# Transposes through DRAM in a hybrid attention and retention step: other run lengths, queues and due times

## The chip, the cores and the metric

The kernel runs on one core of one Trainium2 chip. The metric is the device time of one execution in microseconds (us); smaller is better. A core has TensorE (PE, matrix products; PEld is its weight load), VectorE (DVE), ScalarE (ACT), GpSimd (POOL) and SyncE (SP), which work side by side and wait for each other through semaphores. Transfers are issued into a queue by SyncE, ScalarE or GpSimd and carried out by 16 DMA engines that all queues share. An engine works through its own instructions in order, so one that waits holds up what stands behind it.

## The reference

One layer is applied to 1024 frames of a new stream (the prompt) and to 16 new frames of each of 8 running streams (the sample, 128 rows in all). The frames are normalised and projected to queries, keys, values and gates of 8 stick-breaking heads and 8 retention heads of 128 columns each:

```python
z = q @ k.T * HEAD_DIM ** -0.5
log_beta = log_sigmoid(z)
log_keep = where(strict, log_sigmoid(-z), 0.0)
later = cumsum(log_keep, reverse=True) - log_keep
o_sb = where(strict, exp(log_beta + later), 0.0) @ v
...
scores = (q_r @ k_r.T) * intra
o_r = scores @ v_r + (q_r @ s) * decay_read
s_new = s * gamma ** n + (k_r * decay_write).T @ v_r
...
y = concat(head_rms_norm(o_sb) * g * silu(gate_sb), head_rms_norm(o_r) * g * silu(gate_r))
x = x + rms_norm(y @ w_out) * norm_post
```

In the sample, stick-breaking attention also reads a cache of 1024 old keys and values for each stream and head ("decode"). The new keys, values and retention states are results too. All is float32.

## The kernel before

**Products.** The large projections run as three products of split numbers: each operand is cut into a high and a low part (`split`, L135: ScalarE copies the high part, VectorE subtracts), and high x high, high x low and low x high are added. Weights come in pieces of 256 KB on SyncE's queue (`load_w` L216, `project_rows` L262; in the output stage L969) into four buffers, and are split into four more. All frames of a group are held in SBUF as the moving operand.

**Stages.** First the frames are normalised and turned (to about 120 us). Then two groups of heads follow: group 0 has prompt tiles 0 to 3 and the sample, and runs the decode job of each head; group 1 has prompt tiles 4 to 7, and its stick-breaking rows are up to 1024 keys long. In each group a loop goes over 8 heads and issues six projections for each (plus two wide ones for every pair). The output projection ends the kernel.

**Jobs and ticks.** Everything else of a head is written as generators, "jobs": `ret_branch` with `retention`, `sb_branch` with `stick_breaking`, `decode`, and `Out.finish`. The projections call `tick()` after a few products (in `products` after each of the three products of one slice: two matmuls in group 0, one in group 1). A tick counts a clock up and lets one job that is due go on to its next `yield`; the number yielded is the count of ticks until it is due again. These numbers are the constants `D_...` at the top; where there are two, the first holds for group 0 and the second for group 1. `drain(job)` ticks without products until a job has ended. In the output stage one product group makes `D_OUT`, 35, ticks. `place(inst)` ties an instruction's place behind the last product issued so far; it adds no semaphore. What is not placed is ordered by the compiler on its own reckoning, with the program's order as its priority, as soon as the buffer it writes is free there.

**Round trips.** TensorE's time is spared by transposing elsewhere. VectorE's transpose turns only blocks of 32 x 32, so a larger one goes through DRAM: `turn_out` (L452) stores a tile [128, k x 128] to DRAM as [k, 128, 128] in runs of 512 B; `turn_in` (L458) reads it back with four DMAs, one for each group of 32 partitions, in runs of 128 B, so that the blocks stand in their new places; a VectorE transpose then turns each block and writes its result contiguously. There are five kinds of these trips: the attention weights of a row (`s_be`, in `stick_breaking`: store and reads on GpSimd's queue), those of decode (`s_bd`, store on GpSimd's queue, reads on SyncE's), retention's keys (`s_rk`), and the finished heads of both kinds and of decode (`s_o`); the last two store on ScalarE's queue and read on SyncE's.

**Stick breaking.** For each of four rows of a head the products `z` (L563) give `kp` and `be`; GpSimd masks the diagonal block (L485), VectorE runs the scan (L496) and a product (L497), and the row is stored. The next row's step begins with the reads of this one; two steps on VectorE transposes it (L552) and TensorE multiplies it with the values (L588). Between them lie `D_ZP`, `D_TB` and `D_AV` ticks, and `D_TR` for the last two rows.

**Decode.** 16 pieces of the key cache are loaded (L617, four DMAs of 64 KB each, on GpSimd's queue, three buffers), transposed (L646) and multiplied (L636), `D_ZC` ticks a piece. Then come the trip of the weights (`D_ROW`, `D_DTO`, `D_DTI`, `D_DTR`) and eight pieces of the value cache (L655, 512 KB each, SyncE's queue) in four steps of `D_VC` ticks with two pieces each (L698). The six buffers of tag `kv` are shared by the transposed keys and the values; `load_v()` stands at seven places ahead of the first products.

**Retention.** `ret_branch` sends the keys through DRAM (`D_RO` ticks to the reads, `D_RI` to the transpose L819), scales them, and goes through the tiles `D_RET` ticks apart; L755 is the state's product.

Of the kernel before, what the change touches and what calls it, by code (L numbers as in the profile page):

```python
# [38 lines left out]
D_ZC = 13  # L39
D_ROW = 24  # L40
D_VC = 14
# [4 lines left out]
D_RET = (9, 6)  # L46
D_RO = (21, 23)
D_RI = (19, 26)
D_TO = (26, 23)
D_TB = (33, 33)  # L50
D_TI = (24, 26)
# [9 lines left out]
def tile_hybrid_step(  # L61
# [227 lines left out]
    with ExitStack() as s1:  # L289
# [162 lines left out]
        def turn_out(src, tag, q=nc.scalar):  # L452

            s = scr.tile([src.shape[1], P, P], F32, name=tag)
            q.dma_start(s.rearrange("k q c -> q k c"), src)
            return s

        def turn_in(s, raw, q):  # L458

            for i in range(4):  # L460
                place(q.dma_start(
                    raw[32 * i : 32 * i + 32, :].rearrange("p (k a) -> p k a", a=32),
                    s[:, :, 32 * i : 32 * i + 32].rearrange("k (j b) a -> b (k j) a", b=32),
                ))

        def row_tiles(n, kind):
            if n > 512:
                pool = ip if kind == "r" else zp
                kp = pool.tile([P, n + 1], F32, name="kp", tag=f"kp{kind}")
                be = pool.tile([P, n], F32, name="be", tag=f"be{kind}")  # L470
            else:
                both = zp.tile([P, 2 * n + 1], F32, name="kb", tag=f"{kind}p")
                kp, be = both[:, : n + 1], both[:, n + 1 :]
            nc.vector.memset(kp[:, n : n + 1], 1.0)
            return kp, be
# [26 lines left out]
        class Out:  # L502
# [5 lines left out]
            def done(self, i):  # L508
                sq = op.tile([P, P], F32, name="sq", tag="sq")
                nc.scalar.activation(sq, self.o[:, i, :], AF.Square, accum_out=self.ssq[:, i : i + 1])  # L510

            def finish(self, b, h, gT, oT, dst):
# [4 lines left out]
                s = turn_out(self.o, f"s_o{b}_{h}_{self.nt}")  # L517
                yield D_TO[phase[0]]
                flat = self.o.rearrange("p k d -> p (k d)")
                turn_in(s, flat, nc.sync)  # L520
                yield D_TI[phase[0]]
                n = self.nt * P
                if oT is not None:
                    place(nc.vector.transpose(oT[:, :n], flat))
                    nc.vector.scalar_tensor_tensor(
                        gT[:, :n], oT[:, :n], gains[:, b, h : h + 1], gT[:, :n], ALU.mult, ALU.mult
                    )
                else:
                    for i in range(self.nt):
                        c = slice(i * P, (i + 1) * P)  # L530
                        blk = op.tile([P, P], F32, name="oT", tag="oT", bufs=1)
                        place(nc.vector.transpose(blk, flat[:, c]))
                        nc.vector.scalar_tensor_tensor(
                            gT[:, c], blk, gains[:, b, h : h + 1], gT[:, c], ALU.mult, ALU.mult
                        )
                nc.scalar.dma_start(dst, gT[:, :n])
# [4 lines left out]
        def stick_breaking(tiles, h, q2, keys, rest):  # L541
            out = None
            todo = list(enumerate(tiles))
            lag, kinds = 2, ("psr" if todo[0][1] else ("kp", "be", "cp"))
            rows = []
            for step in range(len(todo) + lag):
                if 0 < step <= len(todo):
                    _, be, turned = rows[step - 1]
                    turn_in(turned, be, nc.gpsimd)
                if step >= lag:  # L550
                    kp, be, _ = rows[step - lag]
                    place(nc.vector.transpose(kp[:, : be.shape[1]], be))  # L552
                if step < len(todo):
# [43 lines left out]
        def decode(h, qs, rest):  # L597
# [15 lines left out]
            def load(m):  # L613
                s, j, c = chunk(m)
                kc = ip.tile([P, 512], F32, name="kc", tag="kc", bufs=3)
                for i in range(4):
                    place(nc.gpsimd.dma_start(  # L617
# [4 lines left out]
                    ))  # L622
# [48 lines left out]
            turned = turn_out(be.rearrange("p (k c) -> p k c", c=P), f"s_bd{h}", nc.gpsimd)  # L671
# [3 lines left out]
            turn_in(turned, be, nc.sync)  # L675
# [3 lines left out]
            place(nc.vector.transpose(kp[:, :n], be))  # L679
# [7 lines left out]
            for k in range(0, 8, 2):  # L687
# [3 lines left out]
                load_v()  # L691
# [21 lines left out]
            ends["d"] = Job(out.finish(0, h, rest["gs"], None, s_ys[h]), 2)  # L713
# [95 lines left out]
        def ret_branch(gi, g, h, rq, rk, rv, rg):  # L809
            nt = len(g["tiles"])  # L810
            rkn = ep.tile([P, 6, P], F32, name="rkn", tag="rkn")

            out = Out(nt, "ro")
            s = turn_out(rk[:, : nt * P].rearrange("p (k t) -> p k t", t=P), f"s_rk{gi}_{h}")
            yield D_RO[phase[0]]
            raw = out.o.rearrange("p k d -> p (k d)")
            turn_in(s, raw, nc.sync)
            yield D_RI[phase[0]]
            place(nc.vector.transpose(rkn.rearrange("p k d -> p (k d)")[:, : nt * P], raw))  # L819
# [5 lines left out]
            ends["r"] = Job(out.finish(1, h, rg, None, s_y[gi][H + h]), 2)  # L825

        def sb_branch(gi, tiles, h, q2, keys, kT, rest, ks):
# [17 lines left out]
            if gi == 0:  # L845
                nc.scalar.dma_start(s_k[h], kT)
# [12 lines left out]
            ends["p"] = Job(out.finish(0, h, rest["sg"], None, s_y[gi][h][:, : 4 * P]), 2)  # L859
# [304 lines left out]
```

## Time and profile before

| | |
|---|---|
| median of 3 runs | 2516.05 us (2508.36 to 2516.53) |
| the profiled execution | 2514.29 us, of which 2512.6 us from the first to the last instruction (the span) |
| mean granted TensorE clock | 0.975 |
| instructions | 40784 |
| DMA | 418.69 MB in 632650 packets, 187776 of them under 512 B |
| queue of SyncE / of GpSimd / of ScalarE | 285.99 MB / 80.80 MB / 49.30 MB |
| share of 16 DMA engines' span | 45.3% / 14.2% / 6.4% |

How to read the views that follow. A page gives the busy time of each engine as a share of the span; an idle engine costs nothing unless it is the one that the others wait for. A line such as `PE pa L588 <- DVE kb L552` in the view of waits says that TensorE's instruction of line 588, which writes `pa`, had waited for VectorE's of line 552; a `q` behind an engine (SPq, POOLq) is its sequencer, which issues DMAs. A line of the timeline gives start, duration, engine, line, operation, `out<-in`, a count, and in brackets the idle time before and what ended it. "To landing" is the time from the issue of a DMA to the arrival of its last byte. The granted clock is the share of TensorE's full speed that the chip allowed.

### The profile page before, as it was taken

Reading aid. Unit: us, or ns where it says so; the run is one execution under the profiler, and the core shown is the slowest. Engines: PE = TensorE matmul, PEld = TensorE weight load, DVE = VectorE, ACT = ScalarE, POOL = GpSimd, SP = SyncE. Lnnn points to the kernel's source line nnn. Section 1 sums busy time; section 2 is a strip of 40 time slices with the busy share of each in tenths; the row PEclk is TensorE's granted clock in tenths of the full one; section 3 lists DMA queues with packets and bytes.
Section 4 is the critical chain, followed back from the end, with each engine's and each line's share of the span. In section 5 each row is a group of like instructions: output and inputs, shape, how many; then the busy total and the mean of one; then the engine's idle time right before and its main releaser. Section 6 shows DMA issues by size and latency. Waiting matters only on the chain. (4 is left out here: it accounts for less than half of the span.)

```text
span 2512.6 us, 40784 instructions
## 1 busy us (share of the span) xinstructions
PE 2377.4 (95%) x14832; PEld 2121.9 (84%) x14832; DVE 1284.7 (51%) x2658; ACT 891.0 (35%) x1925; POOL 704.9 (28%) x1133
## 2 busy tenths in 40 slices
PE   7999898999989989898898999999999997999998
PEld 7999798888979979797677889889889886778787
DVE  7245454454344554445545564555554565464544
ACT  6332232323223232232324333343343443444343
POOL 2134444444434434353331221221211212000000
PEclk9999999998999989999899999999999999999999
DMA  6647867868587776778866556555555557666554
GB/s 233 171 129 164 177 153 171 183 163 167 124 185 172 177 151 152 165 178 193 191 177 160 144 159 151 141 155 136 159 143 144 150 146 180 202 220 201 180 181 139
DMA packets 632650, 418.69 MB, mean 167 GB/s; under 512 B 187776, under 2 KB 575360, under 8 KB 630016
## 3 DMA queue, kind: packets, MB, share of 16 engines
q1 hardware_dynamic: 525424, 285.99, 45.3%
q0 software_dynamic: 36608, 80.80, 14.2%
q10 hardware_dynamic: 70416, 49.30, 6.4%
q8 instruction: 116, 1.90, 0.3%
q14 instruction: 86, 0.70, 0.1%
HBM read 336.24 MB, written 79.69 MB: 166 GB/s over the span
## 5 line engine op out<-in xcount | busy, mean ns | idle before, releaser
L137 DVE TENSOR_TENSOR wl<-wr,wh 128x512 fp32r<-128x512 f32 (+1 forms) x576 | 395.6, 691 | 625.0 <-ACT wh L136 607.9
L230 PE MATMUL acc<-mh,wh 128*128 128x256 f32 (+2 forms) x2304 | 672.6, 344 | 11.3 <-ACT mh L136 6.1
L230 PE MATMUL acc<-ml,wh 128*128 128x256 f32 (+2 forms) x2304 | 675.1, 344 | 0.3 <-DVE ml L137 0.3
L230 PE MATMUL acc<-mh,wl 128*128 128x256 f32 (+2 forms) x2304 | 667.7, 342 | 0.8 <-DVE wl L137 0.8
L136 ACT ACTIVATE wh<-wr 128x512 fp32r<-128x512 f32 (+1 forms) x576 | 357.3, 625 | 778.4 <-PE acc L230 399.5
L230 PEld LDWEIGHTS acc<-mh,wh 128*128 128x128 f32 x2304 | 429.1, 191 | 51.5 <-issue 8.5
L617 POOL DMA_DIRECT2D kc<-cache_sb_k x512 | 330.8, 652 | 503.2 <-DVE kcT L646 263.5
L230 PEld LDWEIGHTS acc<-mh,wl 128*128 128x128 f32 x2304 | 429.2, 191 | 40.1 <-issue 10.5
L230 PEld LDWEIGHTS acc<-ml,wh 128*128 128x128 f32 x2304 | 429.3, 191 | 36.6 <-issue 7.9
L275 PE MATMUL accn<-whn,mh 128*128 128x256 f32 x1152 | 334.6, 290 | 0.5 <-DVE rk L315 0.4
L275 PE MATMUL accn<-wln,mh 128*128 128x256 f32 x1152 | 329.3, 286 | 0.0
L275 PE MATMUL accn<-whn,ml 128*128 128x256 f32 x1152 | 328.5, 286 | 0.0
L275 PEld LDWEIGHTS accn<-whn,mh 128*128 128x128 f32 x1152 | 222.9, 193 | 11.2 <-issue 7.9
L980 PE MATMUL a<-wl,mh 128*128 128x512 f32 (+1 forms) x576 | 220.9, 384 | 9.9 <-DVE wl L137 9.9
L275 PEld LDWEIGHTS accn<-wln,mh 128*128 128x128 f32 x1152 | 223.1, 194 | 4.1 <-issue 3.3
L275 PEld LDWEIGHTS accn<-whn,ml 128*128 128x128 f32 x1152 | 222.9, 194 | 2.1 <-issue 2.1
L981 PE MATMUL a<-wh,ml 128*128 128x512 f32 (+1 forms) x576 | 220.9, 384 | 0.0
L979 PE MATMUL a<-wh,mh 128*128 128x512 f32 (+1 forms) x576 | 218.8, 382 | 0.5 <-DVE so L591 0.5
L137 DVE TENSOR_TENSOR wln<-wrn,whn 128x512 fp32r<-128x512 f32 x128 | 87.7, 689 | 127.6 <-ACT whn L136 119.3
L136 ACT ACTIVATE whn<-wrn 128x512 fp32r<-128x512 f32 x128 | 80.7, 631 | 188.0 <-PE accn L275 74.5
L980 PEld LDWEIGHTS a<-wl,mh 128*128 128x128 f32 x576 | 109.0, 189 | 33.1 <-DVE wl L137 12.4
L836 POOL DMA_DIRECT2D out<-kn x64 | 41.7, 655 | 324.0 <-DVE ou L148 101.0
(203 smaller groups left out, 2750.7 us busy)
## 6 DMA issues: line engine op xcount, KB each, us to landing
wr<-w_in SPq DMA_DIRECT2D x384, 256.0 KB, 3.5
wr<-w_out SPq DMA_DIRECT2D x184, 256.0 KB, 3.5
wrn<-w_in SPq DMA_DIRECT2D x128, 256.0 KB, 3.2
kc<-cache_sb_k POOLq DMA_DIRECT2D x512, 64.0 KB, 4.2
vc<-cache_sb_v SPq DMA_DIRECT2D x64, 512.0 KB, 8.5
xt<-x_prompt SPq DMA_DIRECT2D x8, 1024.0 KB, 5.7
xr<-x_prompt SPq DMA_DIRECT2D x8, 1024.0 KB, 6.1
out<-out ACTq DMA_DIRECT2D x12, 512.0 KB, 2.9
```

Of the source, the lines that this page charges most:

```text
L136: nc.scalar.activation(hi, src, AF.Copy)
L137: nc.vector.tensor_tensor(lo, src, hi.bitcast(F32), ALU.subtract)
L230: last = nc.tensor.matmul(a[:, :m], lhs[:, j, :], rhs[w][:, j, o : o + m], start=(w == 0 and j == 0 and n == 0), stop=(w == KT // WQ - 1 a ...
L275: product[0] = nc.tensor.matmul(a, lhs[q][:, jj, ts], rhs[:, j, :], start=(w == 0 and j == 0 and n == 0 and t % 2 == 0), stop=(w == KT // ...
L617: place(nc.gpsimd.dma_start(kc[32 * i : 32 * i + 32, :].rearrange("p (k d) -> p k d", d=32), cache_k[0, 2 * c + j, s * 512 : (s + 1) * 512 ...
L836: nc.gpsimd.dma_start(k_prompt[0, 0, tiles[0] * P : (tiles[0] + 4) * P, h, ds].rearrange("(j b) a -> b j a", b=32), kn[q, : 4 * P].rearran ...
L979: nc.tensor.matmul(a[:, :width], hi[q][:, j, ts], wh, start=(k == 0), stop=False)
L980: nc.tensor.matmul(a[:, :width], hi[q][:, j, ts], wl, start=False, stop=False)
L981: product[0] = nc.tensor.matmul(a[:, :width], lo[q][:, j, ts], wh, start=False, stop=(k == KT - 1))
```

## The change

Each round trip is written the other way about. `turn_out` stores 32 columns at a time, in runs of 128 B, as [4k, 128, 32], always on GpSimd's queue, in pieces of at most 28 x 128 runs. `turn_in` reads with one DMA in runs of 512 B, and what remains of the permutation is done by VectorE's transpose, whose output is written with a step of four elements (`untangle`). The reads of stick-breaking rows go on SyncE's queue in group 0 and on GpSimd's in group 1; they are issued not at the start of the next step but `D_T1` ticks after its `z`. The stores of `s_y`, `s_ys` and `s_k` move from ScalarE's queue to GpSimd's. Half of each cached key piece is loaded on SyncE's queue; these loads are no longer placed behind a product, and have four buffers. One value load less stands ahead of the first value products. The due times are set anew. Some tiles move to other pools or lose a second buffer, and the rows' two tiles are no longer cut from one.

```diff
-D_ZC = 13
+D_ZC = 12
-D_VC = 14
+D_VC = 18
-D_RET = (9, 6)
-D_RO = (21, 23)
-D_RI = (19, 26)
-D_TO = (26, 23)
-D_TB = (33, 33)
-D_TI = (24, 26)
+D_RET = (7, 6)
+D_RO = (32, 30)
+D_RI = (30, 30)
+D_TO = (40, 40)
+D_T1 = (14, 14)
+D_T2 = (19, 19)
+D_TI = (30, 34)
...
-        def turn_out(src, tag, q=nc.scalar):
-
-            s = scr.tile([src.shape[1], P, P], F32, name=tag)
-            q.dma_start(s.rearrange("k q c -> q k c"), src)
+        def turn_out(src, tag):
+            m = src.shape[1] // 32
+            s = scr.tile([m, P, 32], F32, name=tag)
+            for lo in range(0, m, 28):
+                c = slice(lo, min(lo + 28, m))
+                nc.gpsimd.dma_start(
+                    s[c].rearrange("m q a -> q m a"),
+                    src[:, 32 * c.start : 32 * c.stop].rearrange("q (m a) -> q m a", a=32),
+                )
             return s
...
-        def turn_in(s, raw, q):
-
-            for i in range(4):
-                place(q.dma_start(
-                    raw[32 * i : 32 * i + 32, :].rearrange("p (k a) -> p k a", a=32),
-                    s[:, :, 32 * i : 32 * i + 32].rearrange("k (j b) a -> b (k j) a", b=32),
-                ))
+        def turn_in(s, raw, q=nc.sync):
+            place(q.dma_start(
+                raw.rearrange("p (k c) -> p k c", c=P),
+                s.rearrange("(k i) (b j) a -> (i b) k (j a)", i=4, j=4),
+            ))
+
+        def untangle(dst, raw):
+            place(nc.vector.transpose(dst.rearrange("p (k b j) -> p k j b", j=4, b=32), raw))
...
-                nc.scalar.dma_start(dst, gT[:, :n])
+                nc.gpsimd.dma_start(dst, gT[:, :n])
...
+            def read_back(step):
+                if 0 < step <= len(todo):
+                    _, be, trip = rows[step - 1]
+                    turn_in(trip, be, nc.gpsimd if phase[0] else nc.sync)
+
             for step in range(len(todo) + lag):
-                if 0 < step <= len(todo):
-                    _, be, turned = rows[step - 1]
-                    turn_in(turned, be, nc.gpsimd)
...
-                    place(nc.vector.transpose(kp[:, : be.shape[1]], be))
+                    untangle(kp[:, : be.shape[1]], be)
...
-                    yield D_TB[phase[0]]
-                    be = be[:, :n]
-                    turned = turn_out(be.rearrange("p (k c) -> p k c", c=P), f"s_be{h}_{t}", nc.gpsimd)
-                    rows.append((kp, be, turned))
+                    yield D_T1[phase[0]]
+                    read_back(step)
+                    yield D_T2[phase[0]]
+                    rows.append((kp, be, turn_out(be, f"s_be{h}_{t}")))
...
                     if step >= len(todo):
                         yield D_TR[phase[0]]
+                        read_back(step)
...
-                kc = ip.tile([P, 512], F32, name="kc", tag="kc", bufs=3)
+                kc = ip.tile([P, 512], F32, name="kc", tag="kc", bufs=4)
                 for i in range(4):
-                    place(nc.gpsimd.dma_start(
+                    (nc.gpsimd if i < 2 else nc.sync).dma_start(
...
                 yield D_VC // 2
-                load_v()
+                if k:
+                    load_v()
...
-                nc.scalar.dma_start(s_k[h], kT)
+                nc.gpsimd.dma_start(s_k[h], kT)
```

More of the change, by code (lines that the diff above doesn't have):

```diff
@@ L621, in load @@
                         ),
-                    ))
+                    )
                 return kc
@@ L712, in decode @@
                 yield 3
-            ends["d"] = Job(out.finish(0, h, rest["gs"], None, s_ys[h]), 2)
+            ends["d"] = Job(out.finish(0, h, rest["gs"], s_ys[h]), 2)
         def retention(gi, g, h, out, rq, rk, rkn, rv):
```

60 lines of the change are left out of this document (26 added, 34 removed).

## The prediction

> **What bounds the kernel now.** I read the busy shares on the page first, then a table of busy time by stretch, then TensorE's waits, then the timelines around the two commonest waits. The page says that TensorE is what the kernel runs on:
>
> ```profile
> PE 2377.4 (95%) x14832; PEld 2121.9 (84%) x14832; DVE 1284.7 (51%) x2658; ACT 891.0 (35%) x1925; POOL 704.9 (28%) x1133
> ```
>
> The average hides stages. In the table by stretch the columns are start and end, length, busy time of PE, PEld, DVE, ACT, POOL, then the granted clock, the DMA share and GB/s:
>
> ```profile
> 190.00:1360.00 1170.00, 1090.38 (x7672) 998.34 (x7671) 567.61 (x1285) 345.11 (x797) 480.80 (x798) 0.96 0.75 168
> 1440.00:2060.00 620.00, 617.97 (x3526) 542.07 (x3525) 338.92 (x649) 242.51 (x507) 121.34 (x193) 1.00 0.57 148
> 2060.00:2150.00 90.00, 76.23 (x343) 62.45 (x343) 53.23 (x101) 36.56 (x73) 20.71 (x32) 0.94 0.68 179
> ```
>
> The first group of heads (190 to 1360 us; the only one with the decode job and its cache loads) leaves TensorE idle for 1170 - 1090.4 = 79.6 us, at a clock of 0.96, which is 0.04 x 1170 = 46.8 us more. The second group is idle for 2.0 us of 620 at full clock: nothing can be won there, only lost. So the question is what the change does to some 126 us in the first group. TensorE's waits between 100 and 1350 us name them (total, times, longest):
>
> ```profile
> PE pd L698 <- DMA vc<-cache_sb_v: 32.2, 14, 3.6
> PE pa L588 <- DVE kb L552: 20.8, 9, 5.1
> PE pS L755 <- DVE rkn L823: 8.2, 4, 3.5
> ```
>
> These three are 61 us, and all end in a DMA. The clock goes with them: after the 4.1 us wait that ends at 414.4 us it is 0.57 for four busy microseconds.
>
> ```profile
> 410.00:414.50 4.50, 0.41 (x4) 0.15 (x2) 0.72 (x2) 0.00 (x0) 4.35 (x8) 1.00 0.87 221
> 414.50:418.50 4.00, 4.00 (x19) 4.00 (x20) 2.71 (x9) 0.92 (x3) 3.84 (x6) 0.57 1.36 177
> ```
>
> Over the group 46.8 us of clock stand beside 79.6 us idle, 0.59 for one, so I price an idle microsecond at 1.59 us. That is an estimate from the first row of the table.
>
> **How the waits arise.** The value wait first. On TensorE's timeline the decode products of chunks 0 to 5 (48 matmuls) run in one block, and chunk 6 waits soon behind them; SyncE's timeline has the loads of chunks 6 and 7 going out only after the block has begun, since they reuse the buffers of chunks 0 and 1:
>
> ```profile
> 432.35 2.80 PE L698 MATMUL pd<-vc,kp 128*32 128x256 f32 x48
> ...
> 440.59 0.64 PE L698 MATMUL pd<-vc,kp 128*32 128x256 f32 x8 [3.59 <-DMA vc<-cache_sb_v]
> ```
> ```profile
> 433.05 0.99 SPq L655 DMA_DIRECT2D vc<-cache_sb_v  x2
> ```
> ```profile
> DMA to landing us min/median/max: 5.9/8.5/10.9
> ```
>
> A load that takes 8.5 us is given about 4 us of other products. The second wait: GpSimd had masked rows 2 and 3 by 382.3 us, yet VectorE's scans stand behind other work in its order until 395.8 us, and the store of row 2 leaves at 398.9 us, 16.6 us late.
>
> ```profile
> 380.81 1.50 POOL L485 TENSOR_SCALAR_AFFINE_SELECT kb<-kb 128x128 f32<-128x128 f32 x4
> 398.86 0.76 POOL L455 DMA_DIRECT2D s_be<-kb  x1 [16.55 <-issue]
> ```
> ```profile
> 395.83 2.03 DVE L496 TENSOR_TENSOR_SCAN kb<-kb 128x384 f32<-128x384 f32 x2
> ```
>
> Due times are counted in ticks. A tick of the first group is two products, 0.29 us by two neighbouring starts; one of the second group is one product, 0.23 us.
>
> ```profile
> 405.42 0.45 PE L230 MATMUL acc<-ml,wh 128*128 128x256 f32 x2
> 405.71 0.46 PE L230 MATMUL acc<-mh,wl 128*128 128x256 f32 x2
> ```
> ```profile
> 1768.74 0.40 PE L230 MATMUL acc<-mh,wh 128*128 128x512 f32 x1
> 1768.97 0.40 PE L230 MATMUL acc<-ml,wh 128*128 128x512 f32 x1
> ```
>
> **The change part by part.** *Value loads.* The key phase has 16 steps of 12 ticks instead of 13, so all behind it comes 16 ticks earlier; the four value steps take 18 instead of 14, so the last pair stays at its tick and the first comes 16 - 4 = 12 ticks earlier (3.5 us). The loads of chunks 6 and 7 leave 3.5 to 4.6 us earlier against their use, and the longest wait is 3.6 us. I take five sixths of the 32.2 us away, 27 x 1.59 = **-43 us**. The ends are 0 (the block stays as it is) and -51.
>
> *Retention's key rows.* `D_RO` and `D_RI` give 11 ticks more each, 6.4 us together, against a longest wait of 3.5 us. The wait goes: 8.2 x 1.59 = **-13 us**; `D_RET` of 7 instead of 9 shortens what follows by 22 ticks or more, so the job ends no later.
>
> *Round trips.* Each read is one DMA instead of four, with 512 B runs, and each write has 128 B runs. Durations of the issues (min/median/max ns):
>
> ```profile
> L461 POOL DMA_DIRECT2D kb<-s_be x128: 549/605/709, 203.2 to 1318.0; - x128
> L461 SPq DMA_DIRECT2D ro<-s_o x32: 302/576/3387, 191.7 to 1229.3; - x32
> L461 SPq DMA_DIRECT2D ro<-s_rk x32: 462/1628/3231, 255.7 to 1287.5; - x32
> ```
> ```profile
> L455 POOL DMA_DIRECT2D s_be<-kb x32: 577/757/796, 195.7 to 1305.8; - x32
> ...
> L455 POOL DMA_DIRECT2D s_bd<-be x8: 1022/1024/1032, 259.6 to 1315.0; - x8
> ```
> ```profile
> L617 POOL DMA_DIRECT2D kc<-cache_sb_k x475: 649/649/684, 189.8 to 1282.8; - x159
> ```
>
> GpSimd, per head of the first group: 16 reads of 0.605 us go to SyncE as four, and 32 of its 64 key loads go, 9.7 + 20.8 = 30.5 us less. It gains eight stores that ScalarE issued. An issue grows from 577 ns (128 runs) to 1024 ns (1152 runs), 0.44 ns a run; a 256 KB store with 2048 runs then takes 1.4 us, 0.6 more. Eight such and four longer ones are some 14 us, so GpSimd's load falls by about 16 us of 60. This bears on the second wait: its order is less crowded and the read no longer stands ahead of a store in GpSimd's queue. Whether the compiler then places the scans earlier no row shows; between 0 and 20.8 us I take half, 10.4 x 1.59 = **-16 us**.
>
> Landing times decide what the new writes cost (KB each, median us):
>
> ```profile
> s_bd<-be POOLq DMA_DIRECT2D x8, 576.0 KB, 5.2
> be<-s_bd SPq DMA_DIRECT2D x32, 144.0 KB, 4.6
> ...
> out<-kn POOLq DMA_DIRECT2D x64, 64.0 KB, 3.6
> ...
> s_be<-kb POOLq DMA_DIRECT2D x8, 256.0 KB, 7.4
> kb<-s_be POOLq DMA_DIRECT2D x32, 64.0 KB, 3.5
> ...
> s_be<-kb POOLq DMA_DIRECT2D x8, 64.0 KB, 4.8
> ```
>
> `out<-kn` writes 128 B runs to DRAM from the same queue: 64 KB land in 3.6 us, where 64 KB with 512 B runs take 4.8. The nearest row shows no penalty. The other bound is four such writes in a row for 256 KB, 14.4 us instead of 7.4. The last row of a head has from store to product 22 + 3 + 22 + 3 = 50 ticks, 14.5 us, as before; it needs 0.8 + 7.4 + 0.5 + 3.5 + 0.7 (transpose) = 12.9. Spare: 1.6 us. With 0.6 for the issue and 2 for the landing it is 1 us short, eight times: 8 x 1.59 = **+13 us**; the ends are 0 and, below, +83. The Trainium skill ("DMA: Bandwidth & Descriptors", Specifications) puts the least transfer at line rate at 512 B and says that a smaller one is read, modified and written. By that rule the sum would lie at the far bound, which is the last rival; the 3.6 us row speaks against it.
>
> *Permuting transposes.* VectorE writes every fourth element. No row shows such a write, so I bound it: nothing, or a doubling.
>
> ```profile
> L552 DVE STREAM_TRANSPOSE kp<-be 128x1024 f32<-128x1024 f32 x8 | 9.9, 1236 | 0.0
> ```
>
> Only the last two rows of a head have a product close behind (3 ticks or 0.87 us, 7 ticks or 1.6 us); the lengths here are proportional to the width. Doubled they are short by 0.3 to 0.9 us, 32 times, some 18 us in all; elsewhere 33 ticks and VectorE's idle half hide it. I take nothing, as the element count is the same, and keep +18. The Trainium skill ("SBUF — State Buffer", Door 1: The DMA port swizzle) says that an access in a new 16-byte line pays a penalty, which a step of 16 bytes does every time; by it the sum would be the +18.
>
> *Key loads on SyncE.* 32 issues a head, each like `ro<-s_o` (80 KB in 128 B runs, 0.58 us) or at most 1.6 us like `ro<-s_rk`: 18 to 51 us. Against that, 20 reads of this queue become 5, and 4 rows' reads come over, some 11 issues less, 6 us or more. SyncE waits for buffers most of the time, so this is hidden (0); if not, it is the second rival.
>
> ```profile
> SPq L216 <- DVE wl L137: 251.2, 85, 9.0
> ```
> ```profile
> POOL kc L617 <- DVE kcT L646: 253.4, 54, 13.3
> ```
>
> The second group and the output stage I leave as they are. From 2060 to 2150 us a tick is worth little (35 to each product), and the trip itself is waited for: three issues less, a longer store, 0, between -22 and +22 (13.8 idle x 1.59).
>
> Sum: -43 - 13 - 16 + 13 = -59 us. The profiled execution took 2514.3 us (span 2512.6), 1.8 below the median of 2516.05, so I keep its figure: 2514 - 59 = **2455 us**.
>
> **The rivals.** *The order stays bunched.* Due times only rank instructions; the compiler places them. If the decode block and the late scans stay as they are, retention's 13 us go, and a third of the value wait: 14 + 13 = 27, less 7 for stores, 2494. For it: VectorE's 16.6 us lateness is not the tick plan. Against: GpSimd's lighter load changes what it is placed by. In this form the change largely does not do what it says.
>
> *SyncE's queue blocks.* GpSimd waits 253 us in 54 waits for a key buffer, up to 13.3 us, with nothing urgent behind. On SyncE the weights stand behind. Its longest wait for weight buffers, 9.0 us, costs TensorE no listed wait. If half of the 54 run 1.3 us past what the prefetch covers, 27 x 1.3 x 1.59 = 56 us cancel the gain: 2511. Against it: four key buffers instead of three.
>
> *Short writes are slow* (slower than before). If 256 KB land in 14.4 us, the last row of each first-group head is 5.4 us short: 8 x 5.4 x 1.59 = 69. The decode's 576 KB, stretched alike from 5.2 to 10.1 us, need 1.0 + 10.1 + 0.8 + 4.6 + 1.4 (transpose) = 17.9 us of the 58 ticks (16.8 us) of their trip, 1.1 too much: 14 more. With the value and retention gains of 56 the time is 2514 - 56 + 83 = 2541. It decides from about 13.4 us of landing on, where (13.4 - 9.0) x 8 x 1.59 = 56.
>
> **How the numbers follow.** Forecast 0.55 (own range 2420 to 2485), bunched order 0.13, blocked queue 0.12, slow writes 0.20. 0.3% of 2516, about what a measurement of this kernel can tell from no change, is 7.5 us. Faster: 0.55 + 0.13 = 0.68; same 0.12; slower 0.20. The range goes from 2415 (all of the three waits gone, 2514 - 61.2 x 1.59 = 2417) to 2535 (half of the slow case).
>
> **What would show it.** Right: the two L698 and L588 waits under 10 us each between 190 and 1360 us, the clock there at 0.98 or more, the row stores no longer in pairs 16 us late, and the 256 KB stores landing below 9 us. Wrong: L588 waiting for L552 in most heads with the read's landing just before; or products of L230 waiting for `wl` with SyncE held at L617; or transposes at twice their length. The forecast also fails if the second group, now dense, starts to wait.

## The result, and the profile after

| | before | after |
|---|---|---|
| median | 2512.2 us (2500.53 to 2516.53, 4 runs) | 2483.72 us (2481.82 to 2488.15, 4 runs) |
| ratio | | 0.9896 [0.9857, 0.9935] |
| profiled execution | 2514.29 us, span 2512.6 | 2484.71 us, span 2483.0 |

The change makes the kernel 1.0% faster, 28 us, where 59 were forecast. (Three of the runs below had one slow execution each, of 3300 to 4700 us; their ratios leave it out, and their medians would be about 1 us lower at most without it.) The table of busy time by stretch, asked of the kernel after for the same three stretches (columns as before):

```profile
190.00:1360.00 1170.00, 1120.93 (x7981) 1031.15 (x7980) 635.25 (x1357) 387.13 (x862) 337.77 (x510) 0.98 0.72 177
1440.00:2060.00 620.00, 591.94 (x3250) 511.70 (x3248) 355.01 (x635) 240.36 (x501) 131.38 (x153) 0.98 0.55 143
2060.00:2150.00 90.00, 77.70 (x329) 64.22 (x330) 43.79 (x87) 33.75 (x75) 4.74 (x5) 0.91 0.58 177
```

In the first stretch TensorE's idle time falls from 79.6 to 49.1 us and the clock rises to 0.98: the gain. In the second it rises from 2.0 to 28.1 us, at 0.98 instead of 1.00: a loss where there was nothing to win. The stretches are fixed in time, though, and the stages end earlier after the change: 10.6 of the 28.1 us lie between 2000 and 2060 us, which is output stage by then, and 17.5 before. TensorE's waits between 100 and 1350 us, then after 1360 us, show both:

```profile
PE pd L685 <- DVE kp L471: 37.6, 8, 5.7
PE pa L588 <- DVE kp L471: 5.3, 1, 5.3
```
```profile
PE pa L588 <- DVE kp L471: 32.2, 13, 6.7
PE a L983 <- DVE wl L138: 15.7, 7, 5.5
```

The value wait (32.2 us), the rows' wait of group 0 (20.8) and the wait for retention's keys (8.2) are gone. New is L685, the first product of the decode weights: it waits once a head, eight times, for the decode trip. The waits at L588 are those of group 1's rows, the 5.3 us too (at 1336.90, a row of 1024 keys of its first head). The kernel before had some of them:

```profile
PE pa L588 <- DVE kp L552: 17.4, 9, 5.3
```

With the ends of the stages that the next rows give, they go from 4.8 to 23.3 us in group 1 and from 12.6 to 14.2 in the output stage. There L983 also waits 15.7 us for `wl` (L980 before, 9.9).

How much each stage gave can be read from SyncE's loads, by the last start in three rows: the frames of group 1 (issued when group 0's projections end), the projection weights, and the output weights. Before, then after:

```profile
L197 SPq DMA_DIRECT2D mr<-s_h x16: 319/341/2858, 111.2 to 1227.2; - x16
```
```profile
L216 SPq DMA_DIRECT2D wr<-w_in x384: 367/368/4956, 3.4 to 2040.3; - x192
L969 SPq DMA_DIRECT2D wr<-w_out x192: 327/328/1567, 2044.6 to 2478.4; - x192
```
```profile
L198 SPq DMA_DIRECT2D mr<-s_h x16: 326/344/467, 125.3 to 1159.9; - x16
```
```profile
L217 SPq DMA_DIRECT2D wr<-w_in x384: 367/368/5230, 3.5 to 1998.4; - x192
L972 SPq DMA_DIRECT2D wr<-w_out x192: 327/328/1279, 2001.1 to 2447.9; - x192
```

Group 0 ends 67.3 us earlier. From there to the last projection weight it takes 838.5 us instead of 813.1 (+25.4), and on to the last output weight 449.5 instead of 438.1 (+11.4). So 67 us were won and 37 given back.

**What the new wait is made of.** GpSimd's timeline of one row of 1024 keys in group 1, with VectorE's and TensorE's lines of that row behind it (start, duration, engine, line; in brackets the idle time before and what ended it):

```profile
1744.33 1.00 POOL L465 DMA_DIRECT2D be<-s_be  x1
1750.41 1.59 POOL L458 DMA_DIRECT2D s_be<-be  x1 [5.08 <-DVE wl L138]
1757.40 0.77 POOL L458 DMA_DIRECT2D s_be<-be  x1 [5.40 <-issue]
...
1760.43 0.89 POOL L465 DMA_DIRECT2D be<-s_be  x1 [1.10 <-DMA s_be<-be]
```
```profile
1744.85 1.21 DVE L500 TENSOR_TENSOR be<-be,kp 128x1024 f32<-128x1024 f32 x1
...
1765.68 1.98 DVE L471 STREAM_TRANSPOSE kp<-be 128x1024 f32<-128x1024 f32 x1 [3.80 <-DMA be<-s_be]
```
```profile
1767.71 1.17 PE L588 MATMUL pa<-vn,kp 128*128 128x128 f32 x8 [4.19 <-DVE kp L471]
```

The row is ready at 1744.85 + 1.21 = 1746.06, but its store goes out at 1750.41; its second piece, whose data is the same tile, at 1757.40, with nothing named as its releaser. The landing times of the DMAs in question, asked for one issue each (the read of 1744.33, then the first piece of 1750.41):

```profile
DMA to landing us min/median/max: 5.8/5.8/5.8
```
```profile
DMA to landing us min/median/max: 6.7/6.7/6.7
```

The read lands at 1744.33 + 5.8 = 1750.1, and 0.3 us later the first piece starts; that lands at 1757.1, and 0.3 us later the second starts. (The releaser in the brackets is inferred; neither store reads `wl`, nor below `kp`.) In the decode trip it is the same. The row is ready at 346.01 + 1.34 = 347.35 (VectorE's line first); a key load of 350.97 lands after 8.9 us, at 359.9; the first piece starts at 360.19, lands after 5.6 us at 365.8, and the second starts at 366.09:

```profile
346.01 1.34 DVE L500 TENSOR_TENSOR be<-be,kp 128x1152 f32<-128x1152 f32 x1
```
```profile
350.97 0.66 POOL L617 DMA_DIRECT2D kc<-cache_sb_k  x1
360.19 1.57 POOL L458 DMA_DIRECT2D s_bd<-be  x1 [8.56 <-DVE kp L471]
...
366.09 0.90 POOL L458 DMA_DIRECT2D s_bd<-be  x1 [3.77 <-issue]
```

Four starts, each 0.3 us behind the landing of a DMA that GpSimd had issued before, and no data ties them. It is so in the other heads too: of the 16 stores of group 1's rows of 896 and 1024 keys nine start 0.3 to 0.4 us behind the landing of the row's read that GpSimd had issued before, and behind the other seven it is the next read that starts so long after the landing of the store (of its first piece, where there are two). A first piece has 28 x 128 = 3584 runs. The read of 1744.33 is that of the row before (448 KB in runs of 512 B) and has 7 x 128 = 896, the key load (64 KB in runs of 128 B) 512, a second piece 512 in the row and 1024 in decode, and the kernel is built with a scratch of 4096 for the DMAs that GpSimd issues (`dynamic_dma_scratch_size`). **Ring theory:** each run takes a place in a ring of that size until it has landed, and a store that finds no room holds up GpSimd. Rivals: short runs are slow in themselves, whoever writes them; and the permuting transposes, which did become longer (before, a width of 1024 took 1236 ns):

```profile
L471 DVE STREAM_TRANSPOSE kp<-be 128x1152 f32<-128x1152 f32 x8 | 17.7, 2206 | 23.3 <-DMA be<-s_bd 23.3
L471 DVE STREAM_TRANSPOSE kp<-be 128x1024 f32<-128x1024 f32 x8 | 15.9, 1989 | 22.0 <-DMA be<-s_be 22.0
```

### The profile page after: what moved, and what is told of

Same layout as the page of the kernel before. It is cut to its first block, busy times and chain, and to the rows that moved or that the text cites. A ratio compares the mean times of both kernels' runs of the same rounds, so it can differ in the third digit from the quotient of the medians.

```text
span 2483.0 us, 40526 instructions
## 1 busy us (share of the span) xinstructions
PE 2356.9 (95%) x14832; PEld 2110.4 (85%) x14832; DVE 1346.5 (54%) x2658; ACT 909.4 (37%) x1933; POOL 564.3 (23%) x777
## 4 chain that ended last, share of the span: by engine, by line
PE 64%; issue 13%; DMA 10%; DVE 7%; POOL 3%; ACT 2%; SPq 1%; ACTq 0%; DVEq 0%; POOLq 0%
PE acc L231 36%; PE accn L276 9%; PE a L983 3%; PE a L984 3%; PE a L982 3%; PE pa L588 2%; DMA mr<-s_y 2%; DVE kp L471 2%; DMA be<-s_bd 2%; DMA be<-s_be 1%; PE pd L699 1%; PE z L562 1%; POOL s_be L458 1%; DMA s_bd<-be 1%; DMA mr<-s_ys 1%
## 5 line engine op out<-in xcount | busy, mean ns | idle before, releaser
L231 PE MATMUL acc<-mh,wh 128*128 128x256 f32 (+2 forms) x2304 | 665.8, 342 | 4.3 <-ACT mh L137 2.7
L231 PE MATMUL acc<-ml,wh 128*128 128x256 f32 (+2 forms) x2304 | 662.8, 341 | 0.5 <-DVE ml L138 0.5
L983 PE MATMUL a<-wl,mh 128*128 128x512 f32 (+1 forms) x576 | 223.1, 387 | 15.7 <-DVE wl L138 15.7
L276 PEld LDWEIGHTS accn<-whn,mh 128*128 128x128 f32 x1152 | 220.2, 191 | 10.6 <-issue 8.4
L617 POOL DMA_DIRECT2D kc<-cache_sb_k x256 | 166.9, 656 | 233.0 <-DVE kcT L646 65.9
L499 DVE TENSOR_TENSOR_SCAN kp<-kp 128x640 f32<-128x640 f32 (+6 forms) x72 | 109.7, 1523 | 76.8 <-POOL kp L488 75.8
L983 PEld LDWEIGHTS a<-wl,mh 128*128 128x128 f32 x576 | 110.1, 191 | 39.4 <-DVE wl L138 18.7
```

The lines of the kernel that those rows point to most:

```text
L231: last = nc.tensor.matmul(a[:, :m], lhs[:, j, :], rhs[w][:, j, o : o + m], start=(w == 0 and j == 0 and n == 0), stop=(w == KT // WQ - 1 a ...
L276: product[0] = nc.tensor.matmul(a, lhs[q][:, jj, ts], rhs[:, j, :], start=(w == 0 and j == 0 and n == 0 and t % 2 == 0), stop=(w == KT // ...
L499: nc.vector.tensor_tensor_scan(rev, rev, rev, 1.0, ALU.mult, ALU.bypass)
L617: (nc.gpsimd if i < 2 else nc.sync).dma_start(kc[32 * i : 32 * i + 32, :].rearrange("p (k d) -> p k d", d=32), cache_k[0, 2 * c + j, s * 5 ...
L983: nc.tensor.matmul(a[:, :width], hi[q][:, j, ts], wl, start=False, stop=False)
```

## The experiments

Ratios are to the kernel before, with their 95% intervals.

### What holds the trips back

**Fewer buffers (control), and with them a scratch of 8192.** The larger scratch needs room, so both give up a key buffer and two state buffers.

```diff
-                kc = ip.tile([P, 512], F32, name="kc", tag="kc", bufs=4)
+                kc = ip.tile([P, 512], F32, name="kc", tag="kc", bufs=3)
-                st = ip.tile([P, 2, P], F32, name="st", tag="st", bufs=4)
+                st = ip.tile([P, 2, P], F32, name="st", tag="st", bufs=2)
```
```diff
-    nc = bacc.Bacc("TRN2", target_bir_lowering=False, num_devices=1, dynamic_dma_scratch_size=4096)
+    nc = bacc.Bacc("TRN2", target_bir_lowering=False, num_devices=1, dynamic_dma_scratch_size=8192)
```

> The changed kernel with three key buffers instead of four and two state buffers (st) instead of four; it is the control for the larger descriptor ring, which needs this room. Expected of all theories: 2484 to 2500 us, the waits of L685 and L588 for the transposes as in the changed kernel (37.6 and 37.5 us).

> The same as the control, with room for twice as many descriptors in GpSimd's queue (8192 for 4096 in the kernel's setting). Ring theory (a store of up to 3584 runs waits until what GpSimd issued before has drained, and the second piece waits for the first): the pause of 3 to 5 us ahead of the second pieces goes, and so do most of the waits of L685 and L588 for the transposes; from 75 us to under 35, and the time 30 to 45 us below the control. Rival, short writes (the 128 B runs land slowly by themselves): the pieces go out at once, but land as much later, and the time stays within 8 us of the control. Rival, transposes (the permuting write is what makes the weights late): no change, within 8 us.

The control took 2511.15 us, 1.0006 [0.9984, 1.0028]; the scratch of 8192 took 2427.3 us, 0.9676 [0.9656, 0.9696], 84 us less, about twice what I had expected. L588's and L685's waits went from 35.5 and 33.6 us in the control to 10.3 and 6.0. The ring theory holds, its size was off. The control took 11 us more than I had allowed; its loss (it waits 11.1 us for state rows) shows that buffers are not free here.

**512 B runs.** The stores go out in runs of 512 B and the read takes them as they are; the permutation through DRAM is left out.

```diff
-            m = src.shape[1] // 32
-            s = scr.tile([m, P, 32], F32, name=tag)
...
+            k = src.shape[1] // P
+            s = scr.tile([k, P, P], F32, name=tag)
+            nc.gpsimd.dma_start(s.rearrange("k q c -> q k c"), src.rearrange("q (k c) -> q k c", c=P))
...
-                s.rearrange("(k i) (b j) a -> (i b) k (j a)", i=4, j=4),
+                s.rearrange("k p c -> p k c"),
```

> The changed kernel with stores in runs of 512 B (a quarter of the descriptors, one piece each) and the same single reads in runs of 512 B; the permutation through DRAM is left out, so the transposed tiles hold other values. Ring theory and short-write theory: the store lands 4 to 8 us earlier in group 1 and for the decode weights, the waits of L685 and L588 fall below 35 us in total, and the time is 30 to 45 us below the changed kernel. Transposes theory: the waits stay above 55 us and the time within 12 us.

2405.38 us, 0.9586 [0.9565, 0.9606]; the two waits are 14.1 and 6.2 us. The time fell by 78 us, more than either theory said; both allow the direction.

**Contiguous transposes.** The last part of the permutation is left out.

```diff
-            place(nc.vector.transpose(dst.rearrange("p (k b j) -> p k j b", j=4, b=32), raw))
+            place(nc.vector.transpose(dst, raw))
```

> The changed kernel with contiguous output of the transposes that follow a read; the last part of the permutation is left out, so the tiles hold other values. The transposes fall from 2.2 to 1.37 us (1152 wide) and from 1.99 to 1.24 us (1024). Ring theory: each of some 22 waits is 0.7 to 0.8 us shorter, 75 us become about 58, and the time falls by 12 to 25 us. Transposes theory: the waits fall below 35 us and the time by 30 us or more.

2468.84 us, 0.9843 [0.9812, 0.9874]; waits of 34.1 and 32.5 us. The longer transposes cost about 0.5%, some 13 us (the intervals overlap a little), and are not what holds the rows back.

**One piece per store** (with the scratch of 8192): no cut at 28.

```diff
-            for lo in range(0, m, 28):
-                c = slice(lo, min(lo + 28, m))
+            for lo in range(0, m, 56):
+                c = slice(lo, min(lo + 56, m))
```

> The kernel with the larger ring, and each store in one piece (the limit of 28 raised to 56). Ring theory: one issue less for 24 stores, nothing waits for a first piece; 0 to 12 us below 2427. Rival (a store of 4096 or 4608 runs in one piece waits for the whole ring): 8 us or more above 2427.

2432.91 us, 0.9669 [0.9627, 0.9712]: the same as in pieces. Cutting costs nothing that shows once there is room.

**The kernel before with a scratch of 6144** (two state buffers, one `sq` buffer).

> The kernel before with room for half as many descriptors again in GpSimd's queue (6144 for 4096); two state buffers instead of four and one buffer for the squares make the room. If the ring limits only the changed kernel's stores of short runs, the time stays at 2505 to 2535 (the smaller buffers cost something). If the ring was a limit before the change too (its reads make 1024 descriptors each), the rows that left 16 us late no longer do, and the time falls by 25 us or more.

2512.05 us, 0.9998 [0.9976, 1.002]. TensorE's waits for values (31.1 us) and for the rows of group 0 (19.7) stay, so in the kernel before, with 512 B runs in its stores, the ring isn't what makes them. The smaller buffers, for which there is no control here, may hide a few us (waits for state rows, 5.7 us, are new).

**A scratch of 6144, and stores on ScalarE.** The first keeps the state's buffers and gives up only the fourth key buffer. The second leaves the scratch at 4096 and issues the wide stores (rows over 512 keys, and decode) from ScalarE in one piece, in the same 128 B runs.

```diff
+            q = nc.scalar if m > 16 and "_be" in tag or "_bd" in tag else nc.gpsimd
+            step = m if q is nc.scalar else 28
-            for lo in range(0, m, 28):
-                c = slice(lo, min(lo + 28, m))
-                nc.gpsimd.dma_start(
+            for lo in range(0, m, step):
+                c = slice(lo, min(lo + step, m))
+                q.dma_start(
```

> The changed kernel with GpSimd's DMA scratch at 6144 instead of 4096 and three key buffers instead of four; the state's four buffers stay. Ring theory (a wide store of 3584 runs of 128 B does not fit behind the DMAs that GpSimd issued before it): 6144 holds the store and the reads before it, so the time is that of the 8192 run, 2420 to 2435 us, and since no state buffer is missing, the 10 us of waits for the state's rows are gone too: 2410 to 2430. If the gain of the 8192 run came from anything else in it (three key buffers, two state buffers), the time is 2475 to 2515 us.

> The changed kernel with the scratch at 4096, the wide stores of the stick-breaking rows and of the decode rows issued by ScalarE in one piece. Ring theory: the stores no longer take GpSimd's ring and no longer wait for its earlier DMAs; the waits of L588 and L685 fall from 37.5 and 37.6 us to 10 to 15 each and the time to 2425 to 2445 us. Short-run theory (runs of 128 B cost by themselves, whoever issues them): the same runs are written, so the time stays at 2475 to 2495 us, with the waits at 30 to 38. If ScalarE's own work stands behind the issues, the time is over 2490 us.

2415.84 us, 0.9629 [0.961, 0.9649], and 2418.63 us, 0.9646 [0.9625, 0.9667]. The same loss is taken away in two ways, one of which keeps ring and run length as they were. On GpSimd's timeline of the scratch of 6144, in the same row, both pieces go out together, 0.5 us after VectorE's product has made the row ready at 1701.14 + 1.21 = 1702.35 (VectorE's line second), and beside the read of 1700.63, which lands 5.4 us after its issue, at 1706.0:

```profile
1700.63 0.99 POOL L465 DMA_DIRECT2D be<-s_be  x1
1702.89 2.34 POOL L458 DMA_DIRECT2D s_be<-be  x2 [1.27 <-DVE be L500]
...
1711.92 0.89 POOL L465 DMA_DIRECT2D be<-s_be  x1
```
```profile
1701.14 1.21 DVE L500 TENSOR_TENSOR be<-be,kp 128x1024 f32<-128x1024 f32 x1
```

TensorE's waits there, the three rows of the stages, then the landing times of ScalarE's stores in the other run (KB each, median us) and the wait for its decode trip:

```profile
PE pa L588 <- DVE kp L471: 13.1, 11, 3.5
...
PE pd L685 <- DVE kp L471: 6.9, 5, 2.2
```
```profile
L198 SPq DMA_DIRECT2D mr<-s_h x16: 338/345/467, 122.6 to 1130.3; - x16
```
```profile
L217 SPq DMA_DIRECT2D wr<-w_in x384: 367/368/4794, 3.5 to 1939.7; - x192
L972 SPq DMA_DIRECT2D wr<-w_out x192: 327/328/1112, 1942.4 to 2380.9; - x192
```
```profile
s_bd<-be ACTq DMA_DIRECT2D x8, 576.0 KB, 12.7
...
s_be<-be ACTq DMA_DIRECT2D x8, 512.0 KB, 7.6
```
```profile
PE pd L687 <- DVE kp L473: 16.4, 5, 5.0
```

Against the kernel after, group 0 ends 29.6 us earlier, group 1 takes 809.4 us (29.1 less) and the output stage 441.2 (8.3 less): 67 us, spread over all three stages. The widest stores of short runs do land later (before, with 512 B runs on GpSimd's queue, 576 KB took 5.2 us and 512 KB 4.8; 384 KB took 4.7 us in both). For decode's weights that still costs something: TensorE waits 16.4 us for them, less than the 37.6 of the kernel after and more than the 6.9 with a scratch of 6144.

**Both remedies.**

> The changed kernel with both remedies at once: wide stores on ScalarE's queue and a scratch of 6144. If both remove the same waits (GpSimd's ring), they do not add: 2410 to 2422 us. If the stores on ScalarE also free GpSimd's time, or the ring also held other DMAs, they add: 2390 to 2410 us.

2422.76 us, 0.9645 [0.9606, 0.9685]. They don't add; they take away the same wait.

### Where the gain of group 0 comes from

**The value edit alone**, in the kernel before:

```diff
-D_ZC = 13
+D_ZC = 12
-D_VC = 14
+D_VC = 18
...
-                load_v()
+                if k:
+                    load_v()
```

> The kernel before with the value part of the change alone: 12 ticks a key piece, 18 a value step, and one value load less ahead of the first products. By the prediction's first term the waits of L698 for value loads fall from 32 us to under 10 and the time by some 40 us (2460 to 2480). Rival (the block of six pieces stays where the compiler puts it): the waits stay above 22 us and the time within 10 us of before.

2514.33 us, 1.0005 [0.9984, 1.0026]. TensorE's first wait, there, is as long as before:

```profile
PE pd L699 <- DMA vc<-cache_sb_v: 34.1, 14, 5.1
```

**The key loads put back**, in the kernel after (placed, on GpSimd, three buffers):

> The changed kernel with all key loads on GpSimd's queue again, placed, with three buffers, as before. Ring theory: the key loads' 512 runs each fill the same ring that the stores of short runs need, so the pauses ahead of the decode stores in group 0 grow, and the time is 15 to 50 us above the changed kernel (2500 to 2535); group 1 is unchanged. Rival (SyncE's queue is held up by the key loads): the time falls by 8 us or more.

2619.89 us, 1.0425 [1.0382, 1.0467]; L588 waits 108.0 us. Three buffers alone don't do that (the control, with the loads moved, stood at 1.0006): without the moved key loads the change is a loss. It is far above the 15 to 50 us that I had expected. Of the 108.0 us 37.9 fall after 1400 us, hardly more than in the kernel after (32.2 after 1360), so most of the loss lies in group 0, where the key loads are.

**The key loads alone**, in the kernel before (three buffers), and the two halves of that edit: on two queues but placed as before, and on GpSimd's queue alone but not placed.

```diff
-                    place(nc.gpsimd.dma_start(
+                    (nc.gpsimd if i < 2 else nc.sync).dma_start(
```

> The kernel before with one edit: the key loads go two on GpSimd's queue and two on SyncE's, unplaced; three key buffers as before. If the key loads are the part that gives the change its gain, the block of 48 products falls apart into blocks of 16, the waits for vc and kb go and the time is 2420 to 2470 us. If they pay only together with the moved trips and values, the time stays within 2495 to 2520 us. If SyncE's queue stands behind the key loads (the rival of the forecast), the time is over 2520 us.

> The kernel before with its key loads on two queues, but still placed behind the last product. If dividing the loads between two queues is what gave the 72 us of the unplaced version (GpSimd's queue is free sooner), the time is 2430 to 2455 us. If it is the freedom of place that gave them, the time stays at 2495 to 2515 us.

> The kernel before with its key loads all on GpSimd's queue, no longer placed. If the freedom of place gave the 72 us, the time is 2430 to 2455 us; if the two queues did, 2495 to 2515 us; if it takes both, neither of the two runs is below 2480.

Alone: 2438.51 us, 0.9723 [0.9704, 0.9742], 72 us less than before. Only two queues: 2494.93 us, 0.9928 [0.9903, 0.9953]. Only unplaced: 2490.46 us, 0.9918 [0.9892, 0.9945]. It takes both; by themselves they give 18 and 23 us. TensorE's waits show what each does. First the two rows of TensorE's waits in the placed version, then those in the unplaced one, then in the one with both:

```profile
PE acc L230 <- ACT wh L136: 28.7, 8, 5.0
...
PE accn L275 <- ACT whn L136: 15.9, 4, 5.5
```
```profile
PE pa L588 <- DVE kb L552: 34.5, 12, 5.0
PE pd L698 <- DMA vc<-cache_sb_v: 26.1, 15, 3.6
```
```profile
PE pd L698 <- DMA vc<-cache_sb_v: 3.2, 3, 2.1
...
PE pS L755 <- DVE rkn L823: 0.2, 1, 0.2
```

On one queue the old waits stay (60.6 us where the kernel before has 53.0), so these rows don't say where its 23 us come from. On two queues the values and the rows of group 0 come in time, but with placed loads TensorE waits for weights. A load that waits for its key buffer stands on SyncE's queue ahead of them; the key loads' own rows have `ACT wh L136: 9.9, 4` among those who waited for them, so that much of the 44.6 us is shown to be theirs. Unplaced, the loads wait longer on SyncE in all, yet TensorE's wait for `wh` is 9.7 us there instead of 28.7, and that for `whn` is gone:

```profile
SPq L617 <- DVE kcT L646: 79.7, 36, 7.6
```

What two queues do to the order is seen in one head on TensorE's timeline, first on one queue (unplaced), then on two (unplaced):

```profile
559.67 2.80 PE L698 MATMUL pd<-vc,kp 128*32 128x256 f32 x48
...
567.16 1.08 PE L698 MATMUL pd<-vc,kp 128*32 128x256 f32 x8 [3.56 <-DMA vc<-cache_sb_v]
```
```profile
517.30 1.07 PE L698 MATMUL pd<-vc,kp 128*32 128x256 f32 x16
...
518.79 1.07 PE L698 MATMUL pd<-vc,kp 128*32 128x256 f32 x16
...
524.98 1.07 PE L698 MATMUL pd<-vc,kp 128*32 128x256 f32 x16
...
530.53 1.07 PE L698 MATMUL pd<-vc,kp 128*32 128x256 f32 x16
```

The block of 48 products, behind which the last two value loads were late nearly every time (14 waits in eight heads), falls apart into its four steps of 16. How the queue brings this about isn't shown: GpSimd waits for key buffers as long as before (277.0 us in 60 times against 263.5 in 57, over the whole kernel).

**The value edit on top of the key loads.**

> The kernel before with the key loads of the change (two queues, unplaced) and its edit of the value loads. Theory: the key loads alone dissolve the blocks of 48 products, and the value edit adds nothing: 2433 to 2445 us, as without it. Rival: the value edit pays once the keys are early: 2415 to 2430 us. The forecast gave this edit 43 us.

2458.2 us, 0.9777 [0.9735, 0.982], against 0.9723 [0.9704, 0.9742] without it. It gains nothing there either; the intervals just touch, so a loss isn't certain. Neither of the two ranges that I had given was met.

**The old trips in the kernel after**: stores in 512 B runs, four reads of 128 B runs, contiguous transposes; queues, due times, key and value loads as changed.

```diff
+            for i in range(4):
+                place(q.dma_start(
+                    raw[32 * i : 32 * i + 32, :].rearrange("p (k a) -> p k a", a=32),
+                    s[:, :, 32 * i : 32 * i + 32].rearrange("k (j b) a -> b (k j) a", b=32),
+                ))
```

> The changed kernel with the round trips of the kernel before (one store in runs of 512 B, four reads in runs of 128 B, contiguous transposes), but with the queues, due times, key loads and value loads of the changed one. Ring theory (the permuting stores are what holds the rows back): without them the gain of the key loads shows in full, 2410 to 2450 us. If the permuting trips are themselves worth what the forecast gave them (16 us of bunched rows) and the ring costs little, the time is over the changed kernel's, 2490 to 2520 us. Reads of group 1 on GpSimd then carry the same number of short runs as the stores did, so a loss in group 1 alone would leave 2450 to 2485 us.

2497.77 us, 0.9948 [0.9931, 0.9965]: neither full gain nor the kernel before. My ring theory's number (2410 to 2450) fell. With the rows' reads now on SyncE, four each, TensorE waits for weights and values again:

```profile
PE pd L695 <- DMA vc<-cache_sb_v: 20.1, 7, 4.9
PE acc L231 <- ACT wh L137: 16.5, 16, 2.7
```

So the permuting trips, with one read instead of four, are worth something in this arrangement: 0.9629 with them and room in the ring, 0.9948 without them (0.9896 with them at the same scratch of 4096). What part of that is the count of reads and what the due times wasn't tried apart, and neither were the old trips with a scratch of 6144: their reads in group 1, four of up to 1024 runs each, go out on GpSimd's queue.

**The account in ratios**: 1; with the key loads 0.9723; with the value edit 0.9777; with all the rest and a scratch of 6144 0.9629; with the change's own 4096 (and a fourth key buffer) 0.9896. The version with 6144, 2415.84 us, beats both kernels.

## Why the prediction was right in part and wrong in its total

**The signs of the three waits were right, their cause was not.** The waits for values, retention's keys and late rows of group 0 (-43, -13 and -16) did go, and group 0 gave 67 us where the whole sum was 59. But the step "*Value loads*" failed: that edit alone gave nothing. And the step "*Key loads on SyncE* ... so this is hidden (0)" failed on the other side: I had asked only what the loads cost where they arrive, not what they free where they leave. Alone they give 72 us; with them the block of 48 dissolves, and the wait for `rkn` is 0.2 us without any due time of retention being touched (whether those due times do anything by themselves wasn't tried). Before, I had seen GpSimd wait 253.4 us in 54 waits for key buffers and written that nothing urgent stood behind; the two-queue runs, in which the rows' 20.8 us wait is gone while they stay on GpSimd, speak against that, though not through a shorter wait for buffers.

**The step that made the total wrong** is "The second group and the output stage I leave as they are": 0 was forecast, +25.4 and +11.4 us came. I had named as a condition of failure that the second group might start to wait; it did: 23.3 us at L588 instead of 4.8, and 5.7 us at L685 for the last head's decode trip, which ends there.

**"Landing times decide what the new writes cost"** was the wrong question. The 256 KB stores landed in 8.7 us, within the 9 allowed, and the last rows of group 0 did not wait, where the sum had +13. What counted was when GpSimd could issue a wide store: the decode trip, which had 3.8 us to spare by the landing times before (16.8 less 13.0), made TensorE wait 37.6 us in eight times. The fourth term should have been about +67 (2483.72 less 2415.84, which also gives up the fourth key buffer), for the ring, over all stages. That this lies between the term's ends, 0 and +83, is luck: they were worked out for landing times. Against it all the other parts together gave 96 us, where they were priced at 72.

**The signs.** L698 and L588 under 10 us, a clock of 0.98 and 256 KB stores below 9 us, the signs of being right that I had named for the time between 190 and 1360 us, all came. The total failed all the same: none of them was on a line that had not waited before, as L685.

**Permuting transposes**: taken at 0 with +18 kept as the other end; measured about 13 us. The Trainium skill ("SBUF — State Buffer", Door 1: The DMA port swizzle) says that each step into a new 16-byte line is paid for; the rows agree with its direction, at 1.6 times (1236 to 1989 ns for a width of 1024) and not twice.

**The rivals.** The version with placed loads on two queues waits 44.6 us for weights that the kernel before has in time, as the rival of SyncE's blocked queue said, and 9.9 of them are shown to be the key loads' doing; the change, whose loads aren't placed, hardly has this wait (0.8 us at `wh`). "Short writes are slow" was right that wide stores of short runs land later and wrong that this decides: ScalarE's stores have the same runs, land in 7.6 and 12.7 us, and that kernel takes 2418.63 us. The Trainium skill ("DMA: Bandwidth & Descriptors", Specifications) puts the least transfer at line rate at 512 B; the landing times of the widest stores here agree with it, those of 384 KB show no difference, and the total doesn't hang on it. The order did not stay bunched.

**The range.** The measured time lies inside it, but it is wide. Its lower end (all three waits gone, 2417) is close to what the kernel takes once the ring has room, 2415.84; as the value edit gave nothing and the key loads were priced at 0, that is luck.

## What to carry to other kernels

When work leaves a queue, price what stood behind it there as well as what it meets where it goes: here moving half of the key loads off GpSimd's queue, with their place left free, was worth more than all the rest. When a store is cut into short runs on GpSimd's queue, count the runs of all that GpSimd has in flight, and not only bytes or landing times, and look in the timeline for starts that follow a foreign landing by a fixed 0.3 us with no data between them. A stage that is dense is no neutral ground for a change: a zero for it needs a reason of its own, read from that stage.

## What the runs showed of the hardware

GpSimd's wide stores wait until earlier DMAs of GpSimd have landed, as if each run held one place of a scratch of 4096: 3584 runs did not go out beside a read of 896 or beside a key load of 512, nor a second piece of 512 or 1024 beside them; with 6144 the row's two pieces went out together beside a read of 896. Reads were held up behind wide stores in the same way (768 or 896 runs behind 3584). That the scratch counts runs one for one is worked out from these cases only.

A DMA's issue grew with its runs on GpSimd and not on ScalarE. The rows of the stores in the run with the wide stores on ScalarE and a scratch of 4096, which has both kinds (min/median/max ns; ScalarE's are of 640 to 1024 columns):

```profile
L460 POOL DMA_DIRECT2D s_be<-be x32: 786/977/1195, 159.1 to 1168.1; - x32
L460 ACTq DMA_DIRECT2D s_be<-be x32: 366/367/373, 1241.9 to 1991.0; - x32
```

GpSimd took up to 1195 ns for rows of at most 512 columns, ScalarE 367 ns for rows up to twice as wide.
